# Who computes the last lows of the up weights, the order of a pair's lows, and the down sums spread over the forgetting attention's steps

## The chip, the cores and the metric

The program runs on one core of a Trainium2 chip. The metric is the device time in microseconds (us) of one execution; runs of a kernel are summed up by their median. The core has five engines that run their own instruction streams and wait for each other by semaphores: TensorE (PE in the profile; PEld is its weight load), VectorE (DVE), ScalarE (ACT), GpSimd (POOL) and SyncE (SP), which only issues transfers. DMAs issued by SP and by POOL stand in two queues (q1 and q0 in the profile) of the same 16 DMA engines.

## The reference

The kernel computes a trunk of two layers over 512 tokens of width 1024, in fp32. Layer 0 is a dilated attention and a gated ConvFFN; then one shared key, value and forget gate projection; layer 1 is a forgetting attention and a ConvFFN. What the change touches are the two ConvFFNs and the forgetting attention:

```python
def fox_mixer(xn, w_q, w_o, k, v, c):          # per block of 128 queries:
    s = einsum(q, k[:, :q1]) * scale + (c_t[.., q, None] - c_t[.., None, k])
    p = softmax(where(causal, s, NEG));  out = einsum(p, v[:, :q1])
    ...
def conv_ffn(xn, w_up, cw, cb, w_down):
    a = xn @ w_up                              # 1024 -> 2 * 2816
    a = causal depthwise conv of width 3 over tokens(a) + cb
    gate, val = split(a, 2)
    return (gelu(gate) * val) @ w_down         # 2816 -> 1024
```

## The kernel before

**fp32 products in three.** TensorE multiplies operands of a shorter format (fp32r). Every fp32 operand is split into a high part, its rounding, and a low part, what the rounding left. `mm3` (L275 to L278) makes one product of three matmuls: high by high (L276), high by low of the second operand (L277), low of the first by high (L278).

**Weights.** The class `Weights` (L35 to L99) handles the up, query and output weights as pieces of 128x1024 (512 KB). SP loads a piece into a raw tile `wraw` (L48). ScalarE casts it into the high half of a tile `w` (`high`, L56). The low comes in one of two ways: VectorE subtracts, low = raw - high (`low`, L64); or ScalarE also writes -high into the low half (`high(minus=True)`, L58), and POOL issues a DMA that adds the raw tile to it (`low_added`, L81, an accumulating DMA from tile to tile). `high_added` does L56, L58 and L81 together.

**The up phase of an FFN.** The 2816 hidden channels are 22 chunks of 128 (NF = 22), each with two pieces: gate and value. A loop runs over chunks c = 2 to 21. Chunks in the list SEVEN (the last is 18) are computed with sums of weights and tokens in seven products instead of eight (lines L987 to L1014 combine them on VectorE); the others, 19 to 21 among them, plainly. While chunk c is multiplied, `prepare(c, part)`, called in three places of the chunk (parts 0, 1, 2), prepares the weights of c+1 and c+2; for a plain chunk this is `plain_weights`. The chunk before is finished meanwhile: `taps` (convolution, ScalarE L640, VectorE L641 and L643, twice each), `glu`, `product` (L658), and a store of the chunk's result `hc` to DRAM (`hD`, by POOL, L656).

**The down phase** takes the chunks in 11 pairs (ND = 11). A pair needs the activations `dact`, which SP loads back from `hD` (`pair_load`); sums of them on VectorE (`pair_sums`, L778 to L780), one of which POOL stores; two weights `wraw` and `dact` split in high and low (`pair_highs` by ScalarE, L788; `pair_lows` by VectorE, L792). `mul_one(j, bp)` then has twelve matmuls, four products of `mm3`; the first operand is always `dact`, the second operand is the pair's first weight in the first and the fourth product and the second weight in the second and third. So the lows are needed in this order: the first weight's (second matmul), `dact`'s (third), the second weight's (fifth). The lows of pair 1 are made in the midst of `taps` of the last chunk (21), after the first two VectorE instructions of it, and TensorE multiplies pair 0, then pair 1, at the start of the down phase.

**The down sums.** The weights of a down pair are not multiplied as they are: four combinations of them are stored in DRAM (`dT`) beforehand. The generator `down_sums` does this: SP loads 1 MB into a tile `dsums` (L601 to L603: 512, 256, 256 KB), VectorE subtracts four times (L606 to L609, 128x512 each), and a queue stores two halves of 512 KB (L614). For two of the pairs it runs in the last chunks of the up phase, for four pairs of layer 1 (j = 2 to 5) within the forgetting attention.

**The forgetting attention** is a loop over 16 steps (m = 0 to 15, and two to empty the pipeline). A step is a pair of heads j and two of the four query blocks: blocks 0 and 1 in even steps (i0 = 0), 2 and 3 in odd ones (i0 = 2). A step, in program order: in even steps SP loads the next pair's forget sums (`load_ck`, L1484); TensorE's scores of this step (`f_scores`, L1707); its products with the values for step m-2 (`f_pv`, L1754); softmax numerators (`f_exp`: VectorE L1715, ScalarE L1717) for both blocks; in odd steps the accumulating DMA of the next query weight (`low_added`, L81). Then for both blocks, a = 0 and 1: the biases of the next step by POOL (`f_bias`, L1688 and L1689), a quarter of the query projection of the next pair (`q_part`, TensorE into `q_ps`), the division by the softmax sum (`f_norm`: VectorE L1725, L1727), and transposes of step m-1 (`f_transpose`: TensorE L1739, ScalarE L1741). At the end of an even step the next query weight is loaded and cast (`wraw` by SP L48; L56 and L58). At the end of a step come the down sums: a table says at which steps m a generator of `down_sums` moves on. For j = 2, 3, 4, 5 the load is issued at the end of step 2, 5, 8, 14, the four subtractions stand at the end of step 4, 7, 10, 16, the stores at the end of 5, 8, 11, 17.

Every engine takes its instructions in program order, and no scheduler moves any. SP and POOL run ahead of the others as far as their tiles come free. Tiles come from pools: 16 of 128x2048 (`dsums`, `dact` of a pair, `w`), 10 of 128x1024 (`wraw`, `ck`, `bias` and others), and eight PSUM banks.

Of the kernel before, what the change touches and what calls it, by code (L numbers as in the profile page):

```python
# [1 line left out]

# [10 lines left out]
ALU = mybir.AluOpType  # L13
# [7 lines left out]
NF = DFF // 128  # L21
# [79 lines left out]
def trunk_kernel(ctx, tc, x, norm_gains, w_qkv_a, w_o_a, w_q_b, w_o_b, kv_norm, w_kvf, b_f,  # L101
                 w_up, conv_w, conv_b, w_down, rope, out):
    nc = tc.nc
    act, dve, pool, pe, sp = nc.scalar, nc.vector, nc.gpsimd, nc.tensor, nc.sync
# [8 lines left out]
    def t8(shape, dt=F32, name="t8"):  # L113
        return p8.tile(shape, dt, tag="t8", name=name)
# [47 lines left out]
    dT = [tc.dram_tile([ND, 128, 2048], F32, name=f"dT{l}") for l in range(2)]  # L162
# [45 lines left out]
    W = Weights(nc, new_raw, lambda: t8([128, 2, 1024], F32R, name="w"), pieces)  # L208
# [153 lines left out]
    class Proj:  # L362
# [12 lines left out]
        def step(self, kc, b, hf):  # L375
            ah, al = self.get_act(kc)
            w = self.weight(kc)
            s = slice(b * 128, b * 128 + 128)
            if kc == 0:
                self.banks[b, hf] = bank([128, 512], name="acc")  # L380
            mm3(self.banks[b, hf], ah[:, s], al[:, s], w[0][:, H2[hf]], w[1][:, H2[hf]], kc == 0, kc == self.KC - 1)
# [209 lines left out]
    def down_sums(pairs, place, queue, lag, behind):  # L591


        live, n = [], len(pairs)
        for i in range(n + lag + behind):
            if i < n:
                l, j = pairs[i]
                a, b = place()
                live.append((a, b))
                r = w_down[l][j * 256:j * 256 + 256, :].rearrange("(c p) d -> c p d", p=128)  # L600
                sp.dma_start(a, r[0])  # L601
                sp.dma_start(b[:, 0:512], r[1, :, 512:1024])
                sp.dma_start(b[:, 512:1024], r[1, :, 0:512])  # L603
            if 0 <= i - lag < n:
                a, b = live[i - lag]
                dve.tensor_tensor(a[:, 0:512], a[:, 512:1024], a[:, 0:512], ALU.subtract)  # L606
                dve.tensor_tensor(a[:, 512:1024], b[:, 0:512], a[:, 512:1024], ALU.subtract)
                dve.tensor_tensor(b[:, 0:512], b[:, 0:512], a[:, 0:512], ALU.subtract)
                dve.tensor_tensor(b[:, 512:1024], b[:, 512:1024], b[:, 0:512], ALU.subtract)  # L609
            i -= lag + behind  # L610
            if i >= 0:
                l, j = pairs[i]
                for q, t in enumerate(live[i]):
                    queue.dma_start(dT[l][j, :, q * 1024:q * 1024 + 1024], t)  # L614
            yield
# [15 lines left out]
    def ffn(l, bd, cp, nxt, ahead):  # L631
# [99 lines left out]

        def plain_weights(c):
            for _ in range(2):
                W.high_added()
                yield

        gens = {}

        def step(kind, c):

            if (kind, c) not in gens:
                gens[kind, c] = (plain_weights, first_weights, other_weights)[kind](c)
            next(gens[kind, c], None)

        def prepare(c, part):

            m, n = c + 1, c + 2
            if n >= NF:
                return
            after = c not in SEVEN  # L750
            if m in SEVEN:
                if part == 0 and not after:
                    step(1, m)
                if part == (0 if after else 1) or part == (1 if after else 2):
                    step(2, m)
            if n not in SEVEN:
                if part == 0:
                    step(0, n)
                    step(0, n)
            elif part < 2 or m not in SEVEN:  # L760
                step(1, n)

        acts, one, two, raws, later2 = {}, {}, {}, {}, {}
# [24 lines left out]
                act.copy(w[:, 0], r)  # L788

        def pair_lows(j):  # L790
            for w, r in zip(one[j], raws.pop(j)):
                dve.tensor_tensor(w[:, 1], r, w[:, 0].bitcast(F32), ALU.subtract)  # L792

        def load_two(j):
# [173 lines left out]
        for c in range(2, NF):  # L968
            if c == NF - 4:
                pair_load(0)  # L970
            if c == NF - 3:
                sums = down_sums([(l, ND - 1), (1, 8 + l)], in_one, pool, 1, 0)
                next(sums)
            if c in SEVEN:
# [4 lines left out]
                w = halves.pop(c)  # L979
# [310 lines left out]
    sums = down_sums([(1, 6), (1, 7)], in_two, sp, 1, 3)  # L1290
# [199 lines left out]
    def q_part(j, i):  # L1490

        if j >= 8:
            return
        if i == 0:
            qps[j] = (bank([128, T], name="q_ps"), [t.rearrange("p (k c) -> p k c", k=8) for t in W.get()])
        o, (wh, wl) = qps[j]
        for kc in (2 * i, 2 * i + 1):
            bh, bl = xs(xTq, kc, ALL)
            mm3(o, wh[:, kc, :], wl[:, kc, :], bh, bl, kc == 0, kc == KD - 1)
# [128 lines left out]
    for bp in range(2):  # L1628
        for s in range(2):
            t = slice(bp * 128, bp * 128 + 128)  # L1630
# [135 lines left out]
    def f_out_low(j):  # L1766
        o, t = ops.pop(j), OTb[j // 2]
        dve.tensor_tensor(t[:, 1, j % 2, :], o, t[:, 0, j % 2, :].bitcast(F32), ALU.subtract)

    pairs = [(j, i) for j in range(8) for i in (0, 2)]  # L1770
    po = Proj(8, 4, lambda kc: (OTb[kc // 2][:, 0, kc % 2, :], OTb[kc // 2][:, 1, kc % 2, :]))
    wo = W.n_get + 7
# [7 lines left out]
    f_bias(0, 1)  # L1780
    next(down1)
    M = len(pairs)
    sums = {}
    for j, m in ((2, 2), (3, 5), (4, 8), (5, 14)):
        g = down_sums([(1, j)], in_one, sp, 1, 1)
        for i in (m, m + 2, m + 3):
            sums.setdefault(i, []).append(g)
    for m in range(M + 2):
        live = m < M
        if live:  # L1790
            j, i0 = pairs[m]
            if i0 == 0 and j + 1 < 8:
                load_ck(j + 1)
            s = f_scores(j, i0)
        if m >= 2:
            ju, iu = pairs[m - 2]
            f_pv(ju, iu)
            f_pv(ju, iu + 1)
        if live:
            for a in range(2):  # L1800
                f_exp(j, i0 + a, s[a])
            if i0 == 2 and j < 6:
                W.low_added()
        if m >= 2 and iu == 2:
            f_out_high(ju)
        for a in range(2):
            i = i0 + a
            if live:
                if m + 1 < M:
                    f_bias(pairs[m + 1][0], pairs[m + 1][1] + a)  # L1810
                q_part(j + 1 + (i > 0), (i + 3) % 4)
                if i == 0:
                    q_high(j + 1)
                f_norm(j, i)
            if 1 <= m <= M:
                f_transpose(pairs[m - 1][0], pairs[m - 1][1] + a)
            if 0 <= 2 * m + a - FILL < len(fill):
                po.both(*fill[2 * m + a - FILL])
            if live and (j, i) >= (6, 2):
                W.low()  # L1820
            if live and (j, i) >= (6, 1) and W.n_split < wo + 4:
                W.high()
        if live and i0 == 0:
            q_low(j + 1)
            if j < 6:
                W.high(minus=True)
        if live and i0 == 2 and j:
            f_out_low(j - 1)
        for g in sums.get(m, ()):
            next(g)  # L1830

    f_out_low(7)
    W.ahead, W.ahead_dma = 4, 2
# [48 lines left out]
```

## Time and profile before

| what | value |
|---|---|
| runs of the kernel | 1113.18, 1116.14, 1116.13 us; median 1116.13 |
| the profiled execution | 1115.73 us, its span 1113.6 us |
| busy: PE / DVE / ACT / POOL | 1098.3 / 887.1 / 668.9 / 218.1 us |
| granted TensorE clock | 0.999 of full speed |
| DMA | 241.52 MB, mean 217 GB/s |

The span is the time from the first to the last instruction of the profiled execution; its own time is 2.1 us longer. The page gives each engine's busy time first, then 40 slices of the span, the DMA queues, the chain of work that ended last, and the costliest groups of instructions. A group is named by its line in the kernel, engine, operation and its tiles (out<-in), with the number of instructions, their busy time, the mean of one, and the idle time of the engine before them with what ended it. The views of the trace show single rows: the waits of an engine in total, the chain in order of time, an engine's timeline, and busy times in chosen windows.

### The profile page before, as it was taken

Reading aid. Unit: us, or ns where it says so; the run is one execution under the profiler, and the core shown is the slowest. Engines: PE = TensorE matmul, PEld = TensorE weight load, DVE = VectorE, ACT = ScalarE, POOL = GpSimd, SP = SyncE. Lnnn points to the kernel's source line nnn. Section 1 sums busy time; section 2 is a strip of 40 time slices with the busy share of each in tenths; the row PEclk is TensorE's granted clock in tenths of the full one; section 3 lists DMA queues with packets and bytes.
Section 4 is the critical chain, followed back from the end, with each engine's and each line's share of the span. In section 5 each row is a group of like instructions: output and inputs, shape, how many; then the busy total and the mean of one; then the engine's idle time right before and its main releaser. Section 6 shows DMA issues by size and latency. Waiting matters only on the chain.

```text
span 1113.6 us, 18186 instructions
## 1 busy us (share of the span) xinstructions
PE 1098.3 (99%) x6611; PEld 948.2 (85%) x6611; DVE 887.1 (80%) x1486; ACT 668.9 (60%) x1100; POOL 218.1 (20%) x321
## 2 busy tenths in 40 slices
PE   9999999999999999999999999999999999999997
PEld 6988889899999987888888777889889999987886
DVE  6577878978887679997877778858978887679995
ACT  5544566566566656576565677856566566656573
POOL 1832100211111221000010655500211111221000
PEclk9999999999999999999999999999999999999999
DMA  9469854468788999885762766484468788999962
GB/s 323 139 217 405 345 170 133 106 139 197 178 198 207 239 353 365 322 304 112 209 152 76 237 188 205 148 250 126 112 133 199 177 200 210 235 355 365 325 246 77
DMA packets 186804, 241.52 MB, mean 217 GB/s; under 512 B 11929, under 2 KB 131721, under 8 KB 186714
## 3 DMA queue, kind: packets, MB, share of 16 engines
q1 hardware_dynamic: 169850, 185.00, 50.4%
q0 software_dynamic: 16864, 55.35, 22.8%
q8 instruction: 52, 0.85, 0.3%
q14 instruction: 38, 0.31, 0.1%
HBM read 170.28 MB, written 39.63 MB: 188 GB/s over the span
## 4 chain that ended last, share of the span: by engine, by line
PE 86%; DMA 8%; DVE 2%; ACT 1%; issue 1%; SPq 1%; POOL 0%; DVEq 0%; POOLq 0%; ACTq 0%
PE up L276 10%; PE up L278 10%; PE up L277 10%; PE acc L278 8%; PE acc L276 8%; PE acc L277 8%; DMA dsums<-in_w_down_dram 4%; PE v_ps L276 2%; PE v_ps L277 2%; PE v_ps L278 2%; PE qk_ps L277 2%; PE qk_ps L276 2%; PE qk_ps L278 2%; DMA w<-wraw 2%; PE o_ps L1754 1%; PE first L276 1%
## 5 line engine op out<-in xcount | busy, mean ns | idle before, releaser
L278 PE MATMUL acc<-w 128*128 128x512 f32 (+1 forms) x311 | 120.6, 388 | 3.1 <-DVE w L792 3.1
L276 PE MATMUL acc<-w 128*128 128x512 f32 (+1 forms) x311 | 120.6, 388 | 0.0
L56 ACT CAST w<-wraw 128x1024 fp32r<-128x1024 f32 x96 | 99.4, 1049 | 12.5 <-issue 3.9
L277 PE MATMUL acc<-w 128*128 128x512 f32 (+1 forms) x267 | 103.2, 387 | 0.0
L640 ACT ACTIVATE bb<-up,conv 128x512 f32<-128x512 f32 x80 | 60.1, 776 | 63.0 <-DVE up L1014 42.8
L277 PE MATMUL up<-xbl,w 128*128 128x512 f32 (+1 forms) x280 | 96.3, 344 | 0.0
L277 PE MATMUL up<-xcl,w 128*128 128x512 f32 (+1 forms) x280 | 96.3, 344 | 0.0
L276 PE MATMUL up<-xbh,w 128*128 128x512 f32 (+1 forms) x280 | 96.3, 344 | 0.0
L276 PE MATMUL up<-xch,w 128*128 128x512 f32 (+1 forms) x280 | 96.3, 344 | 0.0
L278 PE MATMUL up<-xbh,w 128*128 128x512 f32 (+1 forms) x280 | 96.2, 344 | 0.0
L278 PE MATMUL up<-xch,w 128*128 128x512 f32 (+1 forms) x280 | 96.2, 344 | 0.0
L64 DVE TENSOR_TENSOR w<-wraw,w 128x1024 fp32r<-128x1024 f32 x58 | 78.8, 1373 | 17.6 <-ACT w L56 17.0
L276 PE MATMUL up<-xsh,w 128*128 128x256 f32 x320 | 90.6, 283 | 0.0
L277 PE MATMUL up<-xsl,w 128*128 128x256 f32 x320 | 90.6, 283 | 0.0
L278 PE MATMUL up<-xsh,w 128*128 128x256 f32 x320 | 90.6, 283 | 0.0
L278 PEld LDWEIGHTS acc<-w 128*128 128x128 f32 x311 | 58.4, 188 | 15.6 <-DVE w L792 3.9
L276 PEld LDWEIGHTS acc<-w 128*128 128x128 f32 x311 | 58.4, 188 | 11.9
L81 POOL DMA_DIRECT2D w<-wraw x38 | 33.0, 867 | 163.9 <-ACT w L58 126.5
L643 DVE SCALAR_TENSOR_TENSOR bb<-up,conv,bb 128x510 f32<-128x510 f32 x80 | 59.9, 749 | 2.8
L788 ACT CAST w<-wraw 128x1024 fp32r<-128x1024 f32 x44 | 45.2, 1050 | 27.3 <-DVE w L792 14.2
L276 PEld LDWEIGHTS up<-xsh,w 128*128 128x128 f32 x320 | 61.4, 192 | 0.0
L277 PEld LDWEIGHTS up<-xsl,w 128*128 128x128 f32 x320 | 61.4, 192 | 0.0
(329 smaller groups left out, 3207.0 us busy)
## 6 DMA issues: line engine op xcount, KB each, us to landing
wraw<-in_w_up_dram SPq DMA_DIRECT2D x88, 512.0 KB, 6.7
w<-wraw POOLq DMA_DIRECT2D x58, 512.0 KB, 6.7
dT<-dsums SPq DMA_DIRECT2D x32, 512.0 KB, 6.1
dsums<-in_w_down_dram SPq DMA_DIRECT2D x22, 512.0 KB, 7.7
dsums<-in_w_down_dram SPq DMA_DIRECT2D x44, 256.0 KB, 7.0
hD<-hc POOLq DMA_DIRECT2D x44, 256.0 KB, 7.7
dact<-hD SPq DMA_DIRECT2D x44, 256.0 KB, 5.8
wraw<-dT SPq DMA_DIRECT2D x22, 512.0 KB, 6.9
```

Of the source, the lines that this page charges most:

```text
L56: self.nc.scalar.copy(pair[:, 0], raw)
L64: self.nc.vector.tensor_tensor(pair[:, 1], raw, pair[:, 0].bitcast(F32), ALU.subtract)
L81: self.nc.gpsimd.dma_start(pair[:, 1], raw, accum_op=ALU.add)
L276: pe.matmul(o, ah, bh, start=first, stop=False, skip_group_check=shared)
L277: pe.matmul(o, ah, bl, start=False, stop=False, skip_group_check=shared)
L278: pe.matmul(o, al, bh, start=False, stop=last, skip_group_check=shared)
L640: act.activation(bb[:, s, :], ps, AF.Identity, bias=cp[:, 3, ch:ch + 1], scale=cp[:, 2, ch:ch + 1])
L643: dve.scalar_tensor_tensor(bb[:, s, 2:], ps[:, :T - 2], cp[:, 0, ch:ch + 1], bb[:, s, 2:], ALU.mult, ALU.add)
L788: act.copy(w[:, 0], r)
L1754: pe.matmul(o[64 * hh:64 * hh + 64, i * 128:(i + 1) * 128], Vt[hd // 8][:, k, (hd % 8) * 64:(hd % 8) * 64 + 64], pT[j, i, hh][:, k, :], st ...
```

## The change

It has three parts.

*The last two up chunks' lows.* `plain_weights` for chunks 20 and 21 of both FFNs casts the high only (no L58) and lets VectorE subtract the low instead of the accumulating DMA. The steps are spread over the parts of `prepare`: high of the first piece in part 0, its low and the second piece's high in part 1, the second low in part 2.

*A pair's lows.* `pair_lows` makes the low of `dact` first, then those of the two weights; before, the weights came first.

*Down sums of the forgetting attention.* A new generator `sums_between` takes the place of `down_sums` there, for j = 2 to 5 at m = 2, 6, 10, 14: loads in the second half (a = 1) of step m, two subtractions at the end of step m+1, two in the first half (a = 0) of step m+2, ahead of `f_norm`, and one store of 1 MB in the second half of step m+2.

```diff
         def plain_weights(c):
             for _ in range(2):
-                W.high_added()
-                yield
+                if c < NF - 2:
+                    W.high_added()
+                else:
+                    W.high()
+                    yield
+                    W.low()
+                if c < NF - 2:
+                    yield
...
             if n not in SEVEN:
-                if part == 0:
-                    step(0, n)
+                step(0, n)
+                if part == 0 and n < NF - 2:
                     step(0, n)
...
         def pair_lows(j):
-            for w, r in zip(one[j], raws.pop(j)):
+            parts = [*zip(one[j], raws.pop(j))]
+            for w, r in (parts[2], parts[0], parts[1]):
                 dve.tensor_tensor(w[:, 1], r, w[:, 0].bitcast(F32), ALU.subtract)
...
+    def sums_between(l, j):
+        t = t8([128, 2, 1024], name="dsums")
+        a, b = t[:, 0], t[:, 1]
+        r = w_down[l][j * 256:j * 256 + 256, :].rearrange("(c p) d -> c p d", p=128)
+        sp.dma_start(a, r[0])
+        sp.dma_start(b[:, 0:512], r[1, :, 512:1024])
+        sp.dma_start(b[:, 512:1024], r[1, :, 0:512])
+        yield
+        dve.tensor_tensor(a[:, 0:512], a[:, 512:1024], a[:, 0:512], ALU.subtract)
+        dve.tensor_tensor(a[:, 512:1024], b[:, 0:512], a[:, 512:1024], ALU.subtract)
+        yield
+        dve.tensor_tensor(b[:, 0:512], b[:, 0:512], a[:, 0:512], ALU.subtract)
+        dve.tensor_tensor(b[:, 512:1024], b[:, 512:1024], b[:, 0:512], ALU.subtract)
+        yield
+        sp.dma_start(dT[l][j].rearrange("p (q d) -> p q d", q=2), t)
+        yield
...
-    sums = {}
-    for j, m in ((2, 2), (3, 5), (4, 8), (5, 14)):
-        g = down_sums([(1, j)], in_one, sp, 1, 1)
-        for i in (m, m + 2, m + 3):
-            sums.setdefault(i, []).append(g)
+    sums, idle = {}, itertools.repeat(None)
+    for j, m in ((2, 2), (3, 6), (4, 10), (5, 14)):
+        g = sums_between(1, j)
+        for i in ((m, 1), (m + 1, 2), (m + 2, 0), (m + 2, 1)):
+            sums[i] = g
...
                 q_part(j + 1 + (i > 0), (i + 3) % 4)
+            next(sums.get((m, a), idle))
+            if live:
                 if i == 0:
                     q_high(j + 1)
                 f_norm(j, i)
...
-        for g in sums.get(m, ()):
-            next(g)
+        next(sums.get((m, 2), idle))
```

TensorE's instructions stand in the same order as before. On the other engines these are the places that matter; the added import shifts all line numbers by one, later additions shift them by up to 27.

First VectorE around the end of chunk 18 in the FFN of layer 0, before the change: taps (L643, L641), the combinations of chunk 18 (L1004 to L1014), `product` (L658), the taps of the next chunk, and the sums of pair 0 (L778).

```order
472 L643 TENSOR_SCALAR bb<-up,conv,bb 128x510
473 L1004 TENSOR_TENSOR up<-up,csum 128x256
474 L1012 TENSOR_TENSOR up<-up,csum 128x256
475 L1014 TENSOR_TENSOR up<-up,csum 128x256
476 L658 TENSOR_TENSOR hc<-bb 128x512
477 L641 TENSOR_SCALAR bb<-up,conv,bb 128x511
478 L643 TENSOR_SCALAR bb<-up,conv,bb 128x510
479 L641 TENSOR_SCALAR bb<-up,conv,bb 128x511
480 L643 TENSOR_SCALAR bb<-up,conv,bb 128x510
481 L778 TENSOR_TENSOR dact<-dact 128x256
```

The same place after the change:

```order
472 L644 TENSOR_SCALAR bb<-up,conv,bb 128x510
473 L65 TENSOR_TENSOR w<-wraw,w 128x1024
474 L1012 TENSOR_TENSOR up<-up,csum 128x256
475 L1020 TENSOR_TENSOR up<-up,csum 128x256
476 L65 TENSOR_TENSOR w<-wraw,w 128x1024
477 L1022 TENSOR_TENSOR up<-up,csum 128x256
478 L659 TENSOR_TENSOR hc<-bb 128x512
479 L642 TENSOR_SCALAR bb<-up,conv,bb 128x511
480 L644 TENSOR_SCALAR bb<-up,conv,bb 128x510
481 L642 TENSOR_SCALAR bb<-up,conv,bb 128x511
482 L644 TENSOR_SCALAR bb<-up,conv,bb 128x510
483 L65 TENSOR_TENSOR w<-wraw,w 128x1024 x2
```

Four lows of up weights (L65, before the shift L64) have come in: the two of chunk 20 around the first combinations of chunk 18, the two of chunk 21 next to each other behind the taps and ahead of the pair's sums. POOL has four rows `L81 DMA w<-wraw` less at this place.

SP in the forgetting attention, steps 2 to 5, before (`ck` is the load at the start of an even step, `wraw` the next weight, `dsums` the loads and `dT` the stores of the down sums):

```order
211 L1484 DMA ck<-cd 128x1024
212 L48 DMA wraw<-in_w_q_b_dram 128x8x128
213 L601 DMA dsums<-in_w_down_dram 128x1024
214 L602 DMA dsums<-in_w_down_dram 128x512
215 L603 DMA dsums<-in_w_down_dram 128x512
216 L1484 DMA ck<-cd 128x1024
217 L48 DMA wraw<-in_w_q_b_dram 128x8x128
218 L614 DMA dT_76<-dsums 128x1024 x2
219 L601 DMA dsums<-in_w_down_dram 128x1024
220 L602 DMA dsums<-in_w_down_dram 128x512
221 L603 DMA dsums<-in_w_down_dram 128x512
222 L1484 DMA ck<-cd 128x1024
```

and after, from the same load of `ck`:

```order
211 L1492 DMA ck<-cd 128x1024
212 L1783 DMA dsums<-in_w_down_dram 128x1024
213 L1784 DMA dsums<-in_w_down_dram 128x512
214 L1785 DMA dsums<-in_w_down_dram 128x512
215 L49 DMA wraw<-in_w_q_b_dram 128x8x128
216 L1492 DMA ck<-cd 128x1024
217 L1793 DMA dT_76<-dsums 128x2048
218 L49 DMA wraw<-in_w_q_b_dram 128x8x128
219 L1492 DMA ck<-cd 128x1024
220 L1783 DMA dsums<-in_w_down_dram 128x1024
221 L1784 DMA dsums<-in_w_down_dram 128x512
222 L1785 DMA dsums<-in_w_down_dram 128x512
```

The three loads of `dsums` stand ahead of the `wraw` that they followed, right behind `ck`; the store stands ahead of the next `wraw`, is one instead of two, and the next load of `dsums` comes behind two loads of `ck` instead of one.

VectorE from an odd to an even step there (before: step 7 to 8; after: the same), where L1715 makes the inputs of the exponentials and L1727 (L1735) divides:

```order
830 L1768 TENSOR_TENSOR OTb_6802<-o_ps,OTb_6802 128x512
831 L606 TENSOR_TENSOR dsums<-dsums 128x512
832 L607 TENSOR_TENSOR dsums<-dsums 128x512
833 L608 TENSOR_TENSOR dsums<-dsums 128x512
834 L609 TENSOR_TENSOR dsums<-dsums 128x512
835 L1715 ISA bias,nm<-s_ps,bias 128x128
836 L1715 ISA nm 128x1
837 L1715 ISA bias,nm<-s_ps,bias 128x128
838 L1715 ISA nm 128x1
839 L1715 ISA bias,nm<-s_ps,bias 128x256
840 L1715 ISA nm 128x1
841 L1715 ISA bias,nm<-s_ps,bias 128x256
```

and after:

```order
833 L1776 TENSOR_TENSOR OTb_6797<-o_ps,OTb_6797 128x512
834 L1787 TENSOR_TENSOR dsums<-dsums 128x512
835 L1788 TENSOR_TENSOR dsums<-dsums 128x512
836 L1723 ISA bias,nm<-s_ps,bias 128x128
837 L1723 ISA nm 128x1
838 L1723 ISA bias,nm<-s_ps,bias 128x128
839 L1723 ISA nm 128x1
840 L1723 ISA bias,nm<-s_ps,bias 128x256
841 L1723 ISA nm 128x1
842 L1723 ISA bias,nm<-s_ps,bias 128x256
843 L1723 ISA nm 128x1
844 L1790 TENSOR_TENSOR dsums<-dsums 128x512
```

Before, all four subtractions stand ahead of the even step's L1715; after, two of them stand there and two behind its four L1715.

More of the change, by code (lines that the diff above doesn't have):

```diff
@@ L1 @@
+import itertools
 from contextlib import ExitStack
```

## The prediction

> **What bounds the kernel now.** First the page: its head and first row.
>
> ```profile
> span 1113.6 us, 18186 instructions
> PE 1098.3 (99%) x6611; PEld 948.2 (85%) x6611; DVE 887.1 (80%) x1486; ACT 668.9 (60%) x1100; POOL 218.1 (20%) x321
> ```
>
> TensorE is busy for 1098 of 1114 us, at full clock throughout, and the change adds or removes no matmul. So the time can move only by what TensorE waits for, and the second view is its waits.
>
> ```profile
> PE q_ps L278 <- DMA w<-wraw: 3.1, 2, 1.8
> PE acc L278 <- DVE w L792: 3.1, 2, 1.6
> PE warm L237 <- DVE zero L232: 1.4, 1, 1.4
> PE qk_ps L277 <- DVE w L64: 1.0, 2, 0.8
> PE s_ps L1707 <- ACT pT L1741: 0.6, 1, 0.6
> ```
>
> Three groups stand in code that the change touches: q_ps (the forgetting attention, waiting for a POOL accumulating DMA), acc (down products, waiting for a pair's lows) and s_ps. Together 3.1 + 3.1 + 0.6 = **6.8 us**, the most that can be won where TensorE's order stays. Third, TensorE's timeline at these five places (start, duration; in brackets the idle time); the last row is the second acc wait, from the chain of waits.
>
> ```profile
> 418.52 0.39 PE L276 MATMUL acc<-w 128*128 128x512 f32 x1
> 418.75 0.39 PE L277 MATMUL acc<-w 128*128 128x512 f32 x1
> 420.71 0.50 PE L278 MATMUL acc<-w 128*128 128x512 f32 x1 [1.57 <-DVE w L792]
> ...
> 636.35 0.50 PE L278 MATMUL q_ps<-xqh,w 128*128 128x512 f32 x1 [1.34 <-DMA w<-wraw]
> ...
> 664.27 0.50 PE L278 MATMUL q_ps<-xqh,w 128*128 128x512 f32 x1 [1.78 <-DMA w<-wraw]
> ...
> 680.25 1.10 PE L1707 MATMUL s_ps<-kst,qst 64*128 64x384 f32 x8 [0.57 <-ACT pT L1741]
> ```
> ```profile
> 1005.73 0.50 PE acc L278
> ```
>
> The matmul at 418.75 follows the one before after 0.23 us, so the third matmul of pair 1, at 420.71, should have begun at 418.98: with 0.16 of refill that place costs 1.73 us, and its twin at 1005.73 (3.1 - 1.57 = 1.5 idle) about 1.65.
>
> **The tail of up, edits A and B.** Fourth view: the chain of waits into 420.71.
>
> ```profile
> 381.23 11.26 DMA dsums<-in_w_down_dram
> 392.50 12.42 DMA dsums<-in_w_down_dram
> 405.01 0.70 DVE dsums L609
> ...
> 414.03 2.56 DMA dact<-hD
> ...
> 417.17 3.50 DVE w L792 x3
> ```
>
> Transfers of 256 KB take 11 and 12 us; VectorE stands for them, and the lows of pair 1 start only at 417.17. VectorE's timeline (the rows before which it stood longest, and a low) and two stretches of the windows:
>
> ```profile
> 381.88 0.43 DVE L1004 TENSOR_TENSOR up<-up,csum 128x256 f32<-128x256 f32 x1 [1.01 <-PE up L278]
> ...
> 386.06 0.43 DVE L1014 TENSOR_TENSOR up<-up,csum 128x256 f32<-128x256 f32 x1 [3.28 <-PE up L278]
> ...
> 399.50 0.69 DVE L606 TENSOR_TENSOR dsums<-dsums 128x512 f32<-128x512 f32 x1 [0.43 <-DMA dsums<-in_w_down_dram]
> 402.80 0.69 DVE L607 TENSOR_TENSOR dsums<-dsums 128x512 f32<-128x512 f32 x1 [2.61 <-DMA dsums<-in_w_down_dram]
> ...
> 405.01 0.69 DVE L609 TENSOR_TENSOR dsums<-dsums 128x512 f32<-128x512 f32 x1 [0.79 <-DMA dsums<-in_w_down_dram]
> ...
> 414.32 0.42 DVE L779 TENSOR_TENSOR dact<-dact 128x256 f32<-128x256 f32 x1 [0.79 <-DMA dact<-hD]
> ...
> 419.44 1.22 DVE L792 TENSOR_TENSOR w<-dact,w 128x1024 fp32r<-128x1024 f32 x1
> ```
> ```profile
> 384.00:396.00 12.00, 12.00 (x60) 10.18 (x59) 9.41 (x16) 7.32 (x9) 3.16 (x5) 1.00 1.06 331
> 396.00:408.00 12.00, 12.00 (x55) 9.94 (x54) 8.00 (x14) 5.08 (x7) 2.87 (x6) 1.00 1.04 324
> ```
>
> The last but one column is the share of the DMA engines: full from 384 to 408, so what is taken off them brings all the rest forward.
>
> *Added.* Four lows by VectorE per FFN at 1.22 us (the row at 419.44 has the same shape) are 4.88 us. The first two (chunk 20) stand around L1004 and L1012: the idle 1.01 and 3.28 us there cover their 2.44, with a shift of 0.2 for L1004, which the 3.28 us before L1014 take up. With that cover gone, another 2.44 would go on top of what follows. The other two (chunk 21) stand at about 390, where VectorE works almost without a gap (9.41 of 12 us, its longest idle time before 386.06), so everything behind is 2.44 late, unless it waits anyway.
>
> *Removed.* Four accumulating DMAs and four ScalarE copies of 1.06 us.
>
> ```profile
> q1 hardware_dynamic: 169850, 185.00, 50.4%
> q0 software_dynamic: 16864, 55.35, 22.8%
> L58 ACT ACTIVATE w<-wraw 128x1024 fp32r<-128x1024 f32 x38 | 40.4, 1063 | 0.0
> DMA to landing us min/median/max: 4.5/6.9/10.8
> ```
>
> The page's queues: q1 took 561 us of all 16 engines for 185 MB, 1.6 us per 512 KB; q0, POOL's, 254 us for 55.35 MB, 2.4 us. Four accumulates of 512 KB hold the engines between 6.4 and 9.6 us. The copies I price at nothing: ScalarE is busy 7.32 and 5.08 of 12 us. VectorE's waits for DMA behind the tail are 0.43 + 2.61 + 0.79 + 0.79 = 4.62 us; 6.4 us less of traffic ahead of them is more than that, so I let them go. So the lows of pair 1 start at 417.17 + 2.44 - 4.62 = 414.99.
>
> *Order of the lows.* Of a pair's twelve matmuls in mul_one, the second needs the low of the first weight, the third the low of dact, the fifth that of the second weight. Before, dact's low is the last of three (1.17 us apart); after, it is the first. With lows from 414.99 the needed ones end near 417.3 and 418.5; TensorE asks at 418.75 (the second matmul) and 0.68 later (the fifth), 419.43. No wait is left. From which start does it hold? The first weight's low must end by 418.75, the start be before 416.4; the second's by 419.43, before 415.9. So VectorE has to come 1.3 us earlier than before, and 2.44 + 1.27 = 3.7 of the 4.62 us must vanish. By itself, with VectorE at 417.17 still, the order turns a wait of 1.73 into 0.85 and 0.4: two matmuls, 0.45 us. What is late next is the release of the accumulators' banks by the taps (L643) right behind these lows, which moves with VectorE. I take **-1.6 us** for each layer, **-3.2** in both, since the second layer has the same code and the same wait; the ends are -3.4 (1.73 + 1.65) and, VectorE late, +4.0 (the first rival).
>
> **The forgetting attention, edit C.** The chain into the two q_ps waits, then SP's own timeline and VectorE's before 680.25:
>
> ```profile
> 628.65 7.66 DMA w<-wraw
> ...
> 654.28 9.95 DMA w<-wraw
> ```
> ```profile
> 628.08 0.32 SPq L1484 DMA_DIRECT2D ck<-cd  x1
> ...
> 631.04 1.72 SPq L601 DMA_DIRECT2D dsums<-in_w_down_dram  x1
> ...
> 653.06 0.45 SPq L601 DMA_DIRECT2D dsums<-in_w_down_dram  x1
> ```
> ```profile
> 673.44 0.86 DVE L606 TENSOR_TENSOR dsums<-dsums 128x512 f32<-128x512 f32 x1
> ...
> 676.13 1.06 DVE L609 TENSOR_TENSOR dsums<-dsums 128x512 f32<-128x512 f32 x1
> ```
>
> The accumulate at 628.65 is issued before 1 MB of dsums (631.04) and takes 7.66 us; that at 654.28, behind a store and 1 MB of dsums, takes 9.95; the fastest, above, 4.5. So what SP put into its queue ahead costs up to 9.95 - 7.66 = 2.3 us.
>
> *First wait (636.35).* The loads move ahead of wraw, right behind ck: issue from 628.4, and thus ahead of the accumulate at 628.65. Price between 0 (the competing bytes are the same, only earlier) and +2.3 (the second case); as the load is half queued when the accumulate starts, and wraw in turn falls behind, I take the value nearer to 0, **+0.9**. Behind it queue POOL's bias operations and TensorE's next products.
>
> *Second wait (664.27).* Loads (653.06) and the one store of 1 MB (before, two of 512 KB) come about 1.3 us earlier, by the order of SP's queue, against the accumulate of 654.28, so that more is drained when it starts; but wraw and ck then also stand ahead. Between -1.78 (gone) and +1.2 (half the first case's price again): **-0.9**.
>
> *Third wait (680.25).* Four sums, 673.44 to 677.19, ahead of the exponentials' inputs at L1715 become none at this step's head: the first two go to the step before (odd), the last two behind L1715. The wait of 0.57 goes, 0.7 with refill; the two sums behind delay L1727 by 1.4 to 1.9 us (at 0.69 and at these rows' durations), for which the transposes wait, so the other end is 1.9 - 0.6 = +1.3. I take **-0.7**, as ScalarE's exponentials, between the two, take as long. Sums at the end of odd steps, 1.4 us, hide behind TensorE's f_pv and q products; steps 2, 6, 10, 14 and their next all have the same form.
>
> Beside them POOL made biases:
>
> ```profile
> 675.54 2.21 POOL L1688 TENSOR_SCALAR bias<-ck,cq 128x512 f32<-128x512 f32 x2
> ```
>
> The sum at 676.13 took 1.06 us, against 0.69 at 399.50. [...]
>
> **Sum.** -3.2 + 0.9 - 0.9 - 0.7 = **-3.9 us**. The profiled execution took 1115.73 us, its span 1113.6 and 2.1 around it: 1111.8. The median shown is 1116.13, 0.4 more; from there 1112.2. I say **1112.0**.
>
> **The rivals.**
> 1. *VectorE becomes the bound of the tail* (slower). If the loads' landing is set by when buffers let SP issue them, not by traffic, the waits of 4.62 stay, and the lows run 2.44 later: 2.44 - 0.45 = +2.0 per layer, +4.0 in both; with the attention at 0, 1119.7. It turns a gain into a loss where less than 2.44 - 0.45 = 2.0 of the 4.62 us vanish. Against it: 11 and 12 us for 256 KB with the engines full. For it: the second transfer of the chain begins where the first lands (381.23 + 11.26 = 392.49), so its issue, too, hung on something. 0.13.
> 2. *The attention gives it back.* The moved loads hold the accumulate of step 1 for 2.3 us and that of step 5 for 1.2: +3.5, -0.7 at the third, and -3.2 in the FFNs: -0.4, 1115.3. For it the row of 9.95; against it that a load needs time to be issued (1.72 us for one at 631.04). 0.20.
> 3. *Less than it says.* About half of VectorE's 4.62 us vanishes and pays just for the lows: TensorE's wait in the tail shrinks only by the order's 0.45 each, and the attention's terms cancel: -0.9, 1114.8. 0.15.
> 4. *The queues share evenly.* Then what stands ahead doesn't matter: the first wait stays as it is, and in the second, an accumulate of 7.66 us like the first's lands at 661.9, before TensorE asks (664.27 - 1.78 - 0.16 = 662.3), so -1.8. With -0.7 and -3.2: -5.7, 1110.0. The 9.95 against 7.66 speak against it. 0.12. [...]
>
> **How the numbers follow.** My forecast, 0.40, spans 1110.5 to 1113.5. A measurement of this kernel can tell about 0.3%, 3.35 us, from no change, so faster means below 1112.8. Faster: 0.32 of the forecast's 0.40, all of rival 4, a bit of 3: 0.46. Slower (above 1119.5): most of rival 1, 0.12. Same: the rest, 0.42. The range takes in the bounds of the unknown costs up to 1117.5 and rival 4 down to 1109.0; it leaves out rival 1 and the far side of 4.
>
> **What would show it.** In the tail: no POOL L81 between 375 and 396; the second dsums transfer below 9 us instead of 12.42; VectorE's idle time for dsums under 1 us; the first L800 of pair 1 before 415.9; no wait acc <- w L800. If that line still stands with VectorE busy before it, rival 1 or 3 is right. In the attention: the accumulate of step 1 at 8 to 9 us (rival 2: near 10; rival 4: under 8); no s_ps wait. What would make it wrong: a new line in TensorE's waits, such as pT_ps waiting for L1735 (the later halves), or up waiting for a low by L65.

## The result, and the profile after

The changed kernel takes **1118.42 us** (median of 7 runs, 1117.87 to 1118.69); the kernel before, in 7 runs beside it, 1114.71. The ratio is 1.0032, 95% interval 1.0020 to 1.0043: 3.7 us slower, where 1112.0 and at most 1117.5 were forecast. The profiled execution took 1118.55 us, its span 1116.8.

The page's head and TensorE's waits after the change:

```profile
span 1116.8 us, 18134 instructions
PE 1100.9 (99%) x6611; PEld 949.9 (85%) x6611; DVE 895.5 (80%) x1494; ACT 660.8 (59%) x1092; POOL 212.8 (19%) x313
```
```profile
PE q_ps L279 <- DMA w<-wraw: 6.5, 3, 4.9
PE warm L238 <- DVE zero L233: 1.4, 1, 1.4
PE acc L278 <- DVE w L65: 1.0, 1, 1.0
PE qk_ps L278 <- DVE w L65: 0.8, 2, 0.5
PE qk_ps L277 <- ACT xah L348: 0.2, 1, 0.2
PE v_ps L278 <- DVE w L1537: 0.2, 1, 0.2
```

Two of the three old groups are gone: no acc wait for a pair's lows, no s_ps wait. The third, q_ps for the accumulating DMA, has grown from 3.1 to 6.5 us, one of its waits to 4.9, and a new acc wait for a low that VectorE makes (L65) has come; it stands in the output projection.

**The tail of up did what was forecast.** VectorE's timeline in layer 0 (start, duration), with no idle time in brackets in these rows, and TensorE at the second and third matmul of pair 1:

```profile
400.78 0.69 DVE L607 TENSOR_TENSOR dsums<-dsums 128x512 f32<-128x512 f32 x1
...
413.75 1.22 DVE L800 TENSOR_TENSOR w<-dact,w 128x1024 fp32r<-128x1024 f32 x1
414.88 2.35 DVE L800 TENSOR_TENSOR w<-wraw,w 128x1024 fp32r<-128x1024 f32 x2
```
```profile
417.91 0.39 PE L278 MATMUL acc<-w 128*128 128x512 f32 x1
418.13 0.39 PE L279 MATMUL acc<-w 128*128 128x512 f32 x1
```

The down sums no longer wait for their loads, the lows of pair 1 start at 413.75 (forecast 414.99), and the third matmul follows the second by 0.22 us. Laid side by side, matmul by matmul, the two traces differ there by -1.73 us in layer 0 and by -1.65 us in layer 1.

**The loss is at step 1's accumulate.** Rows of the chain of waits (start, duration; the first is the accumulating DMA from POOL's issue to its landing), then SP's timeline, then TensorE's:

```profile
627.36 10.42 DMA w<-wraw
637.83 0.79 PE q_ps L279
```
```profile
625.98 0.32 SPq L1492 DMA_DIRECT2D ck<-cd  x1
626.40 0.38 SPq L1783 DMA_DIRECT2D dsums<-in_w_down_dram  x1
626.83 0.42 SPq L1784 DMA_DIRECT2D dsums<-in_w_down_dram  x1
627.30 0.42 SPq L1785 DMA_DIRECT2D dsums<-in_w_down_dram  x1
628.52 0.38 SPq L49 DMA_DIRECT2D wraw<-in_w_q_b_dram  x1
```
```profile
637.83 0.79 PE L279 MATMUL q_ps<-xqh,w 128*128 128x512 f32 x1 [4.91 <-DMA w<-wraw]
```

All three loads of dsums are issued between 626.40 and 627.72 (before: from 631.04), so `ck` and nearly all of the 1 MB stand in SP's queue when POOL issues the accumulate at 627.36, and it takes 10.42 us instead of 7.66. And the matmul at 637.83 takes 0.79 us, not 0.50. The windows show why; the column after the engines' busy times is the granted clock, then the DMA share:

```profile
632.90:636.40 3.50, 0.01 (x1) 0.00 (x0) 1.38 (x4) 1.29 (x4) 0.14 (x1) 1.00 1.08 245
636.40:637.80 1.40, 0.00 (x0) 0.00 (x0) 0.00 (x0) 0.00 (x0) 0.00 (x0) 0.52 0.66 195
637.80:643.20 5.40, 5.37 (x22) 4.45 (x24) 0.19 (x1) 2.14 (x4) 1.78 (x3) 0.50 0.10 36
643.20:645.00 1.80, 1.80 (x30) 1.44 (x28) 1.80 (x7) 1.80 (x4) 0.57 (x1) 0.98 0.59 200
```

While TensorE stands idle its clock is halved, from about 3.5 us after the last matmul until 5.4 us after the wait's end. That is another loss, behind the wait.

Where the time went in the two profiled executions, as the lag of the changed kernel's matmuls behind the same ones of before:

| place (before) | step of the lag, us |
|---|---|
| the first 20 us of the program | -0.8 |
| pair 1's third matmul, layer 0 | -1.73 |
| first q_ps wait, 636.35 | +3.57 |
| half clock behind it | +2.5 |
| second q_ps wait, 664.27 | -0.95 |
| s_ps, 680.25 | -1.0 |
| a third q_ps wait, 691.37 | +0.9 |
| output projection, acc for L65, 710.27 | +1.2 |
| pair 1's third matmul, layer 1 | -1.65 |
| all else, each step below 0.35 | +1.4 |
| end | +3.4 |

Behind the first q_ps wait the lag grows from 1.48 to 3.97 us while the clock is halved, so the half clock costs 2.5 us in this trace; the expectations below count 1.9. Two of the seven timed executions show a mean clock of 0.998. A stretch as long as the 6.8 us of this trace takes 0.003 off the mean by itself, so it can't have come in these two, and they took 1118.18 and 1118.68 us like the rest. How their time divides between wait and clock isn't shown.

### The profile page after: what moved, and what is told of

Its sections match the earlier page's. It is cut to its first block, busy times and chain, and to the rows that moved or that the text cites. A ratio compares the mean times of both kernels' runs of the same rounds, so it can differ in the third digit from the quotient of the medians.

```text
span 1116.8 us, 18134 instructions
## 1 busy us (share of the span) xinstructions
PE 1100.9 (99%) x6611; PEld 949.9 (85%) x6611; DVE 895.5 (80%) x1494; ACT 660.8 (59%) x1092; POOL 212.8 (19%) x313
## 4 chain that ended last, share of the span: by engine, by line
PE 84%; issue 6%; DMA 4%; ACT 3%; DVE 2%; POOL 1%; DVEq 0%; POOLq 0%; ACTq 0%; SPq 0%
PE up L278 13%; PE up L277 13%; PE up L279 13%; PE acc L278 8%; PE acc L277 8%; PE acc L279 8%; DMA w<-wraw 3%; PE qk_ps L278 2%; PE qk_ps L277 2%; PE qk_ps L279 2%; PE first L279 1%; PE first L277 1%; PE first L278 1%; PE v_ps L277 1%; PE v_ps L279 1%
## 5 line engine op out<-in xcount | busy, mean ns | idle before, releaser
L57 ACT CAST w<-wraw 128x1024 fp32r<-128x1024 f32 x96 | 99.1, 1048 | 14.1 <-DMA wraw<-in_w_o_b_dram 5.3
L65 DVE TENSOR_TENSOR w<-wraw,w 128x1024 fp32r<-128x1024 f32 x66 | 88.2, 1351 | 18.4 <-ACT w L57 17.8
L641 ACT ACTIVATE bb<-up,conv 128x512 f32<-128x512 f32 x80 | 60.0, 775 | 67.4 <-DVE up L1022 42.8
L277 PEld LDWEIGHTS up<-xsh,w 128*128 128x128 f32 x320 | 61.4, 192 | 0.0
L279 PEld LDWEIGHTS up<-xsh,w 128*128 128x128 f32 x320 | 61.4, 192 | 0.0
L642 DVE SCALAR_TENSOR_TENSOR bb<-up,conv,bb 128x511 f32<-128x511 f32 x80 | 59.4, 742 | 2.6 <-ACT bb L641 2.6
```

What stands on the lines that cost most here:

```text
L57: self.nc.scalar.copy(pair[:, 0], raw)
L65: self.nc.vector.tensor_tensor(pair[:, 1], raw, pair[:, 0].bitcast(F32), ALU.subtract)
L277: pe.matmul(o, ah, bh, start=first, stop=False, skip_group_check=shared)
L279: pe.matmul(o, al, bh, start=False, stop=last, skip_group_check=shared)
L641: act.activation(bb[:, s, :], ps, AF.Identity, bias=cp[:, 3, ch:ch + 1], scale=cp[:, 2, ch:ch + 1])
L642: dve.scalar_tensor_tensor(bb[:, s, 1:], ps[:, :T - 1], cp[:, 1, ch:ch + 1], bb[:, s, 1:], ALU.mult, ALU.add)
```

## The experiments

Theory A: the loads of dsums, moved in front of the accumulate of step 1, hold it back, and the wait is long enough for the clock to drop. Theory B, the rival: the accumulate's landing is fixed by the traffic there is; TensorE comes earlier out of layer 0's tail and simply waits that much longer, whatever edit C does. All kernels were timed beside the kernel before.

**1. The FFN edits alone** (edits A and B; the table and generator of the down sums as before).

```diff
-    for j, m in ((2, 2), (3, 6), (4, 10), (5, 14)):
-        g = sums_between(1, j)
-        for i in ((m, 1), (m + 1, 2), (m + 2, 0), (m + 2, 1)):
-            sums[i] = g
+    for j, m in ((2, 2), (3, 5), (4, 8), (5, 14)):
+        g = down_sums([(1, j)], in_one, sp, 1, 1)
+        for i in (m, m + 2, m + 3):
+            sums.setdefault(i, []).append(g)
...
```

> The two edits of the FFNs alone; the down sums in the forgetting attention as before. Theory A (the loads of dsums, moved ahead of the accumulate of step 1, hold it back until TensorE has waited so long that its clock drops): the first q_ps wait is 1.5 to 2.5 us, the clock stays full, no acc wait; before's 1114.7 less 3.4, 1111.3 us. Theory B (the landing of that accumulate is fixed by the traffic there is, so TensorE, coming 2.1 us earlier out of layer 0, just waits 2.1 longer, whatever the loads do): the first q_ps wait is 3.4 us or more, and the time 1113.4, or 1115 if the clock drops as well.

Measured: 1112.48 us, ratio 0.9973 (0.9962 to 0.9984), 1.2 us above theory A's number. The waits and the accumulate's row in the chain:

```profile
PE q_ps L279 <- DMA w<-wraw: 2.8, 2, 1.9
...
PE s_ps L1715 <- ACT pT L1749: 0.6, 1, 0.6
```
```profile
627.59 6.39 DMA w<-wraw
```

The accumulate is issued at nearly the same time as after the change, takes 4.0 us less and lands 3.8 us sooner. The first wait is 0.9 us, below the 1.5 to 2.5 expected and shorter than before, although TensorE comes 2 us earlier; the second (1.9) and s_ps (0.6) stand as before. Theory B falls.

**2. Edit C alone** (both FFN edits undone).

```diff
-                if c < NF - 2:
-                    W.high_added()
-                else:
-                    W.high()
-                    yield
-                    W.low()
-                if c < NF - 2:
-                    yield
+                W.high_added()
+                yield
...
-            for w, r in (parts[2], parts[0], parts[1]):
+            for w, r in zip(one[j], raws.pop(j)):
```

> The down sums between steps alone; both edits of the FFNs undone. Theory A: the accumulate lands 1.5 us later than before and TensorE asks when it did before, so the first q_ps wait is about 3 us, below the length at which the clock dropped; with the other places (-0.95, -1.0, +0.9, +1.2) 1116.4 us; if the clock drops after 3 us too, 1118. Theory B: the edit is neutral at the first wait (1.3 us as before) and the time 1114.9.

Measured: 1121.48 us, ratio 1.0055 (1.0042 to 1.0067).

```profile
628.10 10.49 DMA w<-wraw
```
```profile
638.63 0.80 PE L279 MATMUL q_ps<-xqh,w 128*128 128x512 f32 x1 [4.15 <-DMA w<-wraw]
```
```profile
637.40:638.60 1.20, 0.00 (x0) 0.00 (x0) 0.00 (x0) 0.00 (x0) 0.00 (x0) 0.50 1.03 311
638.60:644.00 5.40, 5.37 (x22) 4.45 (x24) 0.18 (x1) 2.13 (x4) 1.77 (x3) 0.50 0.13 27
```

Edit C costs some 6 us by itself. My number was off by 5: I had the landing 1.5 us later than before, and it came 2.3 us later, which made a wait of 4.15 us, and that halves the clock too (2.6 us more of lag behind the wait). The direction is theory A's.

**3. Edit C with its loads behind wraw.**

```diff
-        for i in ((m, 1), (m + 1, 2), (m + 2, 0), (m + 2, 1)):
+        for i in ((m, 2), (m + 1, 2), (m + 2, 0), (m + 2, 1)):
```

> As the change, only the loads of dsums are issued at the end of step m, behind the load of wraw, as before the change, instead of in its second half. Theory A: the first q_ps wait falls from 4.9 to under 2.5 us, the clock stays full, and 3.6 + 1.9 us come back: 1113.0 us. Theory B: the wait stays near 4.9, the clock drops, 1118.4.

Measured: 1110.82 us, ratio 0.9955 (0.9942 to 0.9969), 2 us better than theory A's number.

```profile
627.72 6.57 DMA w<-wraw
```
```profile
PE acc L278 <- DVE w L65: 1.0, 1, 1.0
PE q_ps L279 <- DMA w<-wraw: 1.0, 1, 1.0
```

One place in the program, 7.6 us between the two medians. The accumulate takes 6.57 us, the first wait is 1.04, the second is gone altogether (-1.95 against before), s_ps stays gone. The halves and their places were good; the position of the loads in SP's queue was not.

**4. All query lows by VectorE** in the forgetting attention, with edit C as it is.

```diff
             if i0 == 2 and j < 6:
-                W.low_added()
+                W.low()
...
             if j < 6:
-                W.high(minus=True)
+                W.high()
```

> As the change, and in the forgetting attention too the query weights' lows are made by VectorE (1.2 us each in odd steps) instead of minus copy and accumulating DMA. Both theories: no q_ps wait for DMA (6.5 us in the change), no drop of the clock (1.9 us): 1110.0 us. If VectorE is the bound there, new waits of TensorE for ScalarE or VectorE of about 1 us in each odd step take it back: 1114 to 1116.

Measured: 1108.92 us, ratio 0.9939 (0.9927 to 0.9952), 1 us better than expected. No q_ps wait is left, no drop of the clock, and no new wait of TensorE in the odd steps; what remains is

```profile
PE acc L278 <- DVE w L65: 0.7, 1, 0.7
```

**5 and 6. The FFN edits one by one.** Edit A alone is experiment 1 with `pair_lows` in its old order, edit B alone is experiment 1 with `plain_weights` as before.

> Only the first edit (the last two up chunks' lows by VectorE); order of a pair's lows and down sums as before. If the gain of the tail comes from the traffic that goes (VectorE reaches the lows of pair 1 near 414, and even the last of three ends by 417.5, before TensorE asks at 418.98): both acc waits vanish, 1.73 + 1.65 less, time as with both edits of the FFNs, 1112.0 us. If the order is needed for it: a wait of 0.5 us or more stays at each, 1113.5.

Measured: 1111.46 us, ratio 0.9962 (0.9948 to 0.9975): no less than both edits together, and neither acc wait is there. So edit A is the whole of the FFNs' gain.

> Only the order of a pair's lows; up lows and down sums as before. By the prediction's working 0.45 us less at each of the two acc waits, 1114.4 us, a difference too small for the interval; in the profile, waits for L800 of about 0.75 and 0.4 at the second and fifth matmul of pair 1. If the order does the whole: no acc wait, 1112.0.

Measured: 1114.98 us, ratio 0.9994 (0.9985 to 1.0003). The waits are there, shortened and split:

```profile
PE acc L278 <- DVE w L794: 2.6, 4, 1.1
```
```profile
419.70 0.50 PE L278 MATMUL acc<-w 128*128 128x512 f32 x1 [1.15 <-DVE w L794]
...
420.83 0.50 PE L278 MATMUL acc<-w 128*128 128x512 f32 x1 [0.17 <-DVE w L794]
```

The second and the fifth matmul wait, as the working said, but the second for 1.15 us where about 0.75 was expected. TensorE's idle time at these places is 0.5 us less in both layers together (3.1 to 2.6), and two matmuls instead of one take 0.50 us instead of 0.39 behind a wait (the two rows above): laid beside the same matmuls of before, TensorE is no further ahead behind the two waits than it was in front of them (0.32 against 0.36 us in layer 0, 0.53 against 0.64 in layer 1). No gain from the order alone shows.

**7. Half the load ahead.** Of the first pair (step 2) only 512 KB go ahead of wraw.

```diff
         sp.dma_start(a, r[0])
+        if j == 2:
+            yield
         sp.dma_start(b[:, 0:512], r[1, :, 512:1024])
...
+        if j == 2:
+            sums[m, 2] = g
```

> As the change, but of the first pair's down sums only the first 512 KB are loaded in the second half of step 2, the other 512 KB at its end, behind wraw. If the bytes in front of the accumulate set the wait, it lies in the middle between 1.0 (all behind) and 4.9 (all ahead), 2.5 to 3.2 us; then the clock stays full if what made it drop is the length of the wait: 1118.4 - 2.0 - 1.9 = 1114.5 us. If the clock drops after any wait above 2 us: 1116.4. If being ahead counts and not the bytes: wait 4.5 to 4.9, clock dropped, 1118.

Measured: 1116.04 us, ratio 1.0002 (0.9993 to 1.0011); the profiled execution took 1113.91 at a clock of 1.0, with a transfer of 7.70 us and a wait of 2.18, below the 2.5 to 3.2 expected. The others have clocks of 0.997 and 0.998, and no trace that would show where; so its time, 1.5 us above the 1114.5 expected, tells less than its wait.

```profile
627.52 7.70 DMA w<-wraw
```
```profile
PE q_ps L279 <- DMA w<-wraw: 3.8, 3, 2.2
```

**8. The best of these:** all query lows by VectorE, loads behind wraw, and the third pair's sums in steps 8 to 10.

```diff
-    for j, m in ((2, 2), (3, 6), (4, 10), (5, 14)):
+    for j, m in ((2, 2), (3, 6), (4, 8), (5, 14)):
...
-        for i in ((m, 1), (m + 1, 2), (m + 2, 0), (m + 2, 1)):
+        for i in ((m, 2), (m + 1, 2), (m + 2, 0), (m + 2, 1)):
...
```

> The run with all lows of the forgetting attention by VectorE, with the loads of dsums at the end of a step behind wraw, and the third pair's sums in steps 8 to 10 instead of 10 to 12. If the acc wait for L65 at the start of the output projection (0.7 us) comes from the two sums in step 12 it goes: 1108.9 - 0.8 = 1108.1 us. If it has another cause (the weight's own lateness): 1108.9.

Measured: **1107.91 us**, ratio 0.9929 (0.9916 to 0.9941), 7 us below the kernel before. TensorE's waits in full:

```profile
PE warm L238 <- DVE zero L233: 1.4, 1, 1.4
PE qk_ps L278 <- DVE w L65: 1.0, 2, 0.7
PE v_ps L278 <- DVE w L1537: 0.2, 1, 0.2
PE v_ps L277 <- ACT vp L1414: 0.2, 1, 0.2
```

The acc wait for L65 is gone. Experiment 3 has the loads behind too and keeps it, so it went with the new place of the third pair; the rows of 706.71 to 715.21 below put it down to the two sums in step 12, ahead of the output projection's lows on VectorE.

**9. Three quarters ahead** (768 KB of the first pair's 1 MB): experiment 7 with the `yield` one load later.

> As the change, but of the first pair's down sums 768 KB are loaded in the second half of step 2 and the last 256 KB at its end, behind wraw. If the bytes ahead set the wait (1.0 us with none, 2.2 with 512 KB, 4.9 with 1 MB ahead), the first q_ps wait is 3.2 to 3.8 us. It lies between the waits after which the clock stayed full (2.2) and halved (4.2): a halved clock here puts the point below 3.8 us and the time at 1117.2, a full one above 3.2 us and the time at 1115.5.

Measured: 1116.44 us, ratio 1.0018 (1.0008 to 1.0027); the profiled execution 1115.80 at a clock of 1.0.

```profile
627.67 9.11 DMA w<-wraw
```
```profile
636.83 0.50 PE L279 MATMUL q_ps<-xqh,w 128*128 128x512 f32 x1 [3.59 <-DMA w<-wraw]
```

The wait is 3.59 us, in the range that the bytes gave, and the clock stays full in this execution. The median lies 0.9 us above the 1115.5 expected for a full clock; the other executions have clocks from 0.996 to 0.998, and no trace.

**10. One low by VectorE**: the loads stay ahead, only step 1's accumulate is replaced.

```diff
-                W.low_added()
+                W.low() if m == 1 else W.low_added()
...
-                W.high(minus=True)
+                W.high(minus=m > 0)
```

> As the change, but the one accumulate of step 1 is replaced by a low by VectorE; the loads of dsums stay ahead. If the wait for this accumulate, with the halved clock that follows it, is the whole loss of the change against its FFN part, both go (5.1 + 1.9 us): 1111.4 us, clock full. If the loads ahead harm in another way too (wraw late, VectorE late), a wait of TensorE under another name takes its place at about 635: 1115.

Measured: 1111.02 us, ratio 0.9961 (0.9946 to 0.9976). The wait and the drop of the clock go with this one transfer, and the loads ahead do no other harm of size here: two other q_ps waits remain, 1.0 us together.

**11. The first pair's loads behind**, the others ahead.

```diff
-        for i in ((m, 1), (m + 1, 2), (m + 2, 0), (m + 2, 1)):
+        for i in ((m, 2 if j == 2 else 1), (m + 1, 2), (m + 2, 0), (m + 2, 1)):
```

> As the change, but the loads of the first pair alone (step 2) go behind wraw; those of the third and fourth stay ahead of it. The first q_ps wait falls to 1.0 us and the clock stays full (3.9 + 1.9 us), the others remain (second 0.8, third 0.7): 1112.5 us. If instead all the loads together count, the waits stay above 2 us: 1115 or more.

Measured: 1112.67 us, ratio 0.9983 (0.9973 to 0.9992). The first wait is 1.5 us and the clock full. The other two waits stay (0.65 and 1.13 us), as they do not in experiment 3. Matmul by matmul this trace falls behind that of experiment 3 by 0.5 us at the first wait, 0.8 at the second and 1.3 at the third, 2.9 in all, so the second and third pairs' loads ahead make most of the difference; between the medians it is 1.9 us.

## Why the prediction was wrong

*The base* was 1116.13, the median of three runs; the seven beside the change have 1114.71. So the forecast step of -3.9 us is to be laid beside a measured +3.7.

*The FFN terms were right.* Forecast -3.2, measured -1.73 - 1.65 = -3.4, by the mechanism named: traffic goes, VectorE's waits of 4.62 us vanish, and the four lows are paid from them. Experiment 5 confirms it alone. Rival 1, VectorE as the bound, didn't happen: its idle time of 4.62 us went with the accumulating DMAs. The order's own 0.45 us per layer did not show in experiment 6.

*The second and third waits were right too:* -0.95 for -0.9, and -1.0 for -0.7. At the second the mechanism was the one named: the accumulate (issued at 658.49, TensorE being 4.0 us later by then) took 8.75 us instead of 9.95, as the store of 1 MB and the first load were issued 5.1 and 2.7 us ahead of it instead of 3.1 and 1.2. At the third the wait went.

*The step that failed is "First wait (636.35)", the choice of +0.9 between 0 and +2.3.* It measured +3.57, and another +2.5 of half clock followed, which no term had. The mechanism stood in the text, as rival 2 (its second wait, +1.2, did not come); the size was wrong three times over. Of the 7.3 us between the sum of -3.9 and the trace's +3.4, this place makes 2.7 + 2.5.
- The price of what is ahead. I took the value near 0, "as the load is half queued when the accumulate starts". It was queued all but entirely: SP issued three loads in 1.3 us (626.40 to 627.72), each in about 0.4 us, so the 1.72 us of the row at 631.04 was no price of an issue; and the first of them went out 1.0 us ahead of the accumulate, where the working had 628.4 against 628.65. The transfer became 2.8 us longer (10.49 against 7.66, edit C alone) or 4.0 (10.42 against 6.39, with and without C beside the FFN edits). Even my upper end, +2.3 from the row of 9.95, was too low.
- The sum. I added the FFNs' -1.6 of layer 0 and the first wait's price as if both counted. TensorE came 2.1 us earlier to this wait, but the transfer's issue moved by only 1.3 us (628.65 to 627.36). So the +3.57 is 2.76 of longer transfer and 0.8 of TensorE's gain that the issue did not follow. Where a wait ends with a transfer, time that TensorE won before it counts only as far as the landing moves too: in experiment 1 it did (issue 1.1 us earlier, transfer 1.3 us shorter), and nothing was lost.
- The clock. No term of the sum had it, as no row of the kernel before had a wait of more than 1.78 us. The drop costs 2.5 us behind the wait. Experiments 3, 10 and 11 take away the long wait in three ways, and the clock stays full in each.

*Not priced at all,* 2.1 us together, were the waits where C's other loads and sums meet something: the third pair's loads ahead of the accumulate of 685 us (+0.9, gone with the loads behind), and two sums in step 12 ahead of an output weight's low (+1.2, gone with the sums in step 10). VectorE and TensorE there, after the change:

```profile
706.71 1.12 DVE L1790 TENSOR_TENSOR dsums<-dsums 128x512 f32<-128x512 f32 x1
707.87 0.77 DVE L1791 TENSOR_TENSOR dsums<-dsums 128x512 f32<-128x512 f32 x1
...
713.93 1.22 DVE L65 TENSOR_TENSOR w<-wraw,w 128x1024 fp32r<-128x1024 f32 x1
```
```profile
715.21 0.50 PE L278 MATMUL acc<-w,OTb 128*128 128x512 f32 x1 [1.02 <-DVE w L65]
```

VectorE goes from the sums through the next step's work to the low at 713.93 with little idle time, and the output projection takes that low as soon as it is there. The sentence "steps 2, 6, 10, 14 and their next all have the same form" passed over what stands around those steps.

*Rival 4,* an even share of the queues, falls. With 0, 512, 768 and 1024 KB ahead of it the same accumulate took 6.57, 7.70, 9.11 and 10.42 us, and the wait was 1.0, 2.2, 3.6 and 4.9. That is 1.1 us more for the first 512 KB, then 1.4 and 1.3 for 256 KB each, where 256 KB by the page's average hold the engines for 0.8 us: beyond the first half, what is ahead is paid for in full and more. With an even share what stands ahead would not matter, and here 1 MB ahead and 1 MB behind differ by 3.9 us (10.42 against 6.57).

The traces show where these 3.9 us lie. Counted from its issue, the accumulate's first packet starts 1.5 us later in experiment 3 (at 629.20) and 5.2 us later after the change (at 632.57); from that packet to the landing it takes 5.1 and 5.2 us. So between these two it hardly runs slower; it starts later. The queues (packets, MB, share of the 16 engines) after the change, from 627.40 to 632.50 and from there to the landing, and in experiment 3 from 629.20 to the landing:

```profile
q1 hardware_dynamic: 403, 1.20, 87.6%
```
```profile
q0 software_dynamic: 144, 0.52, 49.9%
q1 hardware_dynamic: 1132, 0.74, 45.8%
```
```profile
q0 software_dynamic: 144, 0.52, 73.4%
q1 hardware_dynamic: 721, 0.39, 25.4%
```

For 5.1 us POOL's queue (q0) moves nothing while SP's (q1) works off `ck` and `dsums`, which were issued ahead. No taking of turns between the two shows until 1.33 of their 1.57 MB are through (0.14 MB from 625.98 to 627.40 and the 1.20 of the first row). Whether the engines keep this order or POOL's packets come to them late isn't shown by these runs.

## What to carry to other kernels

A DMA that an engine will wait for must be judged by what is queued on the other queues when it is issued: with a 1 MB load issued 1 us ahead of it instead of 1.6 us behind (experiment 3), TensorE lost 6.4 us at this place, 3.9 of wait and 2.5 of slow clock, and moving it back made the same edit a gain. Time won before such a wait counts only as far as the transfer's landing moves with it. And a replaced transfer can be worth more than it looks: four 1.2 us subtractions per FFN on a busy VectorE were cheaper than four accumulating DMAs in a stretch where the DMA engines were full (share 1.06 and 1.04 from 384 to 408 us before the change).

## What the runs showed of the hardware

The clock. Waits of TensorE of 4.15 and 4.91 us halved its granted clock, the waits of 1.04, 2.18 and 3.59 us at the same matmul in experiments 3, 7 and 9 did not. It fell 2.9 us (edit C alone) and 3.5 us (the change) after the last matmul, and was full again 5.6 and 5.4 us after the start of the first one behind the wait. In both it was halved for the same 6.83 us (637.41 to 644.24 and 636.45 to 643.28). The time without a matmul does not by itself tell when it falls: the 2.9 us after which it fell in edit C alone are less than the 3.59 us of experiment 9, through which it stayed full. What decides it isn't shown. The 5.4 us at half clock, in which TensorE was busy for 5.37, cost 2.5 us, nearly half of them.

VectorE's sum at 706.71, beside POOL's bias operations of 705.93 to 707.29, took 1.12 us, against 0.69 for the same shape at 400.78. How much of the 1.2 us at the output projection this made isn't separated by the runs.
